# Layer norm and RWKV head norm of a two-layer encoder trunk with their GpSimd steps moved to VectorE and ScalarE

## The chip, the cores and the metric

The kernel runs on one core of one Trainium2 chip. The metric is the device time of one execution in microseconds (us), the median of several runs. The engines of the core work on instruction queues of their own: TensorE (PE; PEld is its weight load), VectorE (DVE), ScalarE (ACT), GpSimd (POOL), and SyncE (SP), which here issues the DMA transfers.

## The reference, cut to what matters

Two layers run over 2560 tokens (2048 of one request and 512 of another) of width 1024. Both layers end with an output projection, a gated residual and a layer norm over the 1024 channels; layer 1 also has RWKV-7 heads, whose output gets a norm over the 64 channels of each head.

```python
def layer_norm(x, g, b, eps=1e-5):
    mu = jnp.mean(xf, axis=-1, keepdims=True)
    var = jnp.mean(jnp.square(xf - mu), axis=-1, keepdims=True)
    return ((xf - mu) * lax.rsqrt(var + eps) * g + b).astype(x.dtype)
...
# end of rwkv7_time_mix
mu = jnp.mean(o, axis=-1, keepdims=True)
var = jnp.mean(jnp.square(o - mu), axis=-1, keepdims=True)
o = ((o - mu) * lax.rsqrt(var + RWKV_LN_EPS)).reshape(bsz, seq, D_W) * lnx_w + lnx_b
return (o + bonus.reshape(bsz, seq, D_W)) * jax.nn.silu(g.astype(jnp.float32))
...
# end of each layer
y = jnp.concatenate([c_out, d_out], axis=-1) @ w_out
return residual_post_norm(x, gate, y, ln_g, ln_b)   # layer_norm(ALPHA * x + (1 + gate) * y)
```

## The kernel before

The tokens are cut into 5 blocks of 512. Values that go into a matmul at higher precision are split in two: ScalarE copies x to a rounded `hi`, and another engine writes `lo = x - hi`; the matmul is then a sum of products of the parts (three for an output projection).

The stages follow one another: layer 0 (input projection, HGRN2 and GLA heads), its output projection `out_proj(0)` (1493 to 1745 us of the profiled execution), the input projection of layer 1 (to some 2640 us), the core of layer 1 with attention and the RWKV scan (to some 3800 us), and `out_proj(1)` (to the end).

`out_proj` works on tiles of 128 tokens, 20 in all. For a tile it loads `oh` and `ol` (the parts of the heads' output) and `xt` (the residual), does 48 matmuls of 512 columns into two halves `pp` (three buffers), and for each half runs three DVE instructions: `y = pp * gt`, `y = ALPHA * xt + y`, and the norm's statistics. Then `ln_tail` follows for the whole row: a few instructions on one column for mean and reciprocal deviation, the normalization in one DVE instruction (L357), and multiply by `lng` and add of `lnb`, the lower 512 channels on DVE and the upper 512 on POOL. In `out_proj(0)` the result is written to memory, transposed on PE, modulated (`h`), split (`h1s`, whose `lo` is computed on POOL) and written as input of layer 1; in `out_proj(1)` it is the output.

`rwkv_post` is the head norm. It runs once for each of 4 pairs of heads and each block, 20 times, on tiles of 128 channels by 512 tokens (all named `ptmp`): two loads, their sum (POOL), split (ACT, POOL), a matmul with `cmean` that subtracts the head's mean, copy and square (ACT, DVE), split (ACT, POOL), a matmul with `bmean` for the variance, `Ln` and `Exp` on ACT for the reciprocal root, a square on POOL and two DVE instructions that refine it, multiply and affine step on DVE, add of the bonus (POOL), multiply by the gate (DVE), and `out_split` (ACT, POOL) with two writes to `o_scr`.

Work is interleaved by generators in lanes: each `tick()` advances the first generator of every lane by one `yield`. The four `rwkv_post` of the block `self.first` (block 1) run one after the other in the lane "post" at the end of the core of layer 1; the other 16 are fed by `feed1` in four lanes F0 to F3 while `out_proj(1)` runs its tiles, beginning with block 1; the tiles of a block begin, in program order, only after its four posts. The pool of `ptmp` has 20 buffers there. The final order of the instructions on each engine is set by a scheduler with a time model of its own (`schedule_with_timeline_sim=True`), which works from the program order as priority; each engine then runs its queue in that fixed order. `ln_exp()` loads the ACT function set that holds both `Ln` and `Exp` once ahead of these stages.

The helpers `tt` (two tensors, L113), `stt` (tensor, scalar, tensor; L116), `ts` (tensor, two scalars; L123) and `act` (L110) issue the instructions, so that most rows bear their lines.

Of the kernel before, what the change touches and what calls it, by code (L numbers as in the profile page):

```python
# [11 lines left out]
F32R = mybir.dt.float32r  # L12
I32 = mybir.dt.int32
BF16 = mybir.dt.bfloat16
AF = mybir.ActivationFunctionType
ALU = mybir.AluOpType
# [24 lines left out]
class Common:  # L41
# [303 lines left out]
    def ln_tail(self, b, t, y, st, lng, lnb, emit_tile, pools):  # L345
        nc = self.nc
        sm = pools[1]
        mv = sm.tile([128, 2], F32, tag="mv", name="mv")
        nc.vector.bn_aggr(mv, st)
        rs = sm.tile([128, 1], F32, tag="rs", name="rs")  # L350
        self.act(rs, mv[:, 1:2], AF.Ln, bias=self.eps5)
        self.act(rs, rs, AF.Exp, scale=-0.5)
        va = sm.tile([128, 1], F32, tag="va", name="va")
        self.ts(va, mv[:, 1:2], 1e-5, rs, ALU.add, ALU.mult)
        self.ts(va, va, rs, -0.5, ALU.mult, ALU.mult)
        self.stt(rs, va, 1.5, rs, ALU.add, ALU.mult)
        self.ts(y, y, mv[:, 0:1], rs, ALU.subtract, ALU.mult)  # L357
        h = slice(0, 512)
        g = slice(512, 1024)
        self.tt(y[:, h], y[:, h], lng[:, h], ALU.mult)  # L360
        self.tt(y[:, g], y[:, g], lng[:, g], ALU.mult, nc.gpsimd)
        self.tt(y[:, h], y[:, h], lnb[:, h], ALU.add)
        self.tt(y[:, g], y[:, g], lnb[:, g], ALU.add, nc.gpsimd)
        yield
        yield from emit_tile(b, t, y, pools)


class Even(Common):
# [197 lines left out]
        self.out_split(y, col, b)  # L566
        yield

    def out_split(self, y, col, b, pool=None):
        nc = self.nc  # L570
        yh, yl = (pool.tile([128, NB], F32R, tag=x, bufs=1 + (pool is not self.ap), name=x) if pool else self.wt(x, dt=F32R) for x in ("yh", "yl"))
        self.act(yh, y, AF.Copy)
        self.tt(yl, y, yh, ALU.subtract, nc.gpsimd)
        nc.sync.dma_start(out=self.o_scr[b, 0, :, col], in_=yh[:].bitcast(F32))
        nc.sync.dma_start(out=self.o_scr[b, 1, :, col], in_=yl[:].bitcast(F32))

# [267 lines left out]
class Odd(Even):  # L844
# [659 lines left out]
    def rwkv_post(self, p, b, pool, bufs):  # L1504

        nc = self.nc
        t1 = lambda dt=F32: pool.tile([128, NB], dt, tag="ptmp", bufs=bufs, name="ptmp")
        o, c = t1(), t1()
        nc.sync.dma_start(out=o, in_=self.acc_scr[0, p, b])
        nc.sync.dma_start(out=c, in_=self.acc_scr[1, p, b])  # L1510
        yield
        yield
        yield
        self.tt(o, o, c, ALU.add, nc.gpsimd)
        yield
        yield
        yield
        parts = self.split(o, t1(F32R), t1(F32R))
        yield
        yield  # L1520
        yield
        yield
        ps = self.psum()
        self.mm2(ps, self.cmean, parts)
        nc.scalar.copy(c, ps)
        self.tt(o, c, c, ALU.mult)
        parts = self.split(o, t1(F32R), t1(F32R))
        yield
        yield
        yield  # L1530
        yield
        ps = self.psum()
        self.mm2(ps, self.bmean, parts)
        rs = t1()
        self.act(rs, ps, AF.Ln, bias=self.eps64)
        self.act(rs, rs, AF.Exp, scale=-0.5)
        u = t1()
        self.tt(u, rs, rs, ALU.mult, nc.gpsimd)
        nc.sync.dma_start(out=o, in_=self.bv_scr[p, b])
        yield  # L1540
        self.stt(u, ps, 64e-5, u, ALU.add, ALU.mult)
        self.stt(rs, u, 3.0, rs, ALU.subtract, ALU.mult)
        self.tt(c, c, rs, ALU.mult)
        self.ts(c, c, self.rvw[:, p:p + 1], self.rv[:, 7, p:p + 1], ALU.mult, ALU.add)
        nc.sync.dma_start(out=rs, in_=self.g_scr[p, b])
        yield
        self.tt(c, c, o, ALU.add, nc.gpsimd)
        self.tt(c, c, rs, ALU.mult)
        yield
        self.out_split(c, 4 + p, b, pool)  # L1550
        yield

    def feed1(self, order, pool):
# [206 lines left out]
```

## Time and profile before

| | us |
|---|---|
| median of 3 runs | 4163.66 (4152.8 to 4171.17) |
| the profiled execution | 4167.95 |
| its span, first to last instruction | 4166.2 |
| PE busy in it | 3743.6 (90%) |
| DVE busy | 2838.6 (68%) |
| ACT busy | 2149.8 (52%) |
| POOL busy | 1145.3 (27%) |

Busy times are merged: overlapping instructions of one engine count once. Busy time of an instruction runs from its start to its end, and so holds time in which it is held up after its start.

### The profile page before, as it was taken

What the parts mean: (1) busy time and instruction counts of PE and PEld (TensorE: products, weight loads), DVE (VectorE), ACT (ScalarE), POOL (GpSimd) and SP (SyncE); (2) the same over time, 40 slices, a digit from 0 to 9 for tenths busy, and PEclk for the clock granted to TensorE, in tenths of its full rate; (3) what the DMA queues carried; (4) which work ended last, traced back from release to release, by engine and by line L of the source; (5) the groups of instructions that cost most, each with busy time, mean ns of one, the idle gap of its engine ahead of it and who ended that gap; (6) DMA issues with size and microseconds to landing.
All of it is one profiled execution on the core that took longest, in us unless ns stands there. A gap on an engine that the chain in (4) does not pass through costs nothing. (4 is left out here: it accounts for less than half of the span.)

```text
span 4166.2 us, 75101 instructions
## 1 busy us (share of the span) xinstructions
PE 3743.6 (90%) x27864; PEld 3067.3 (74%) x27864; DVE 2838.6 (68%) x6393; ACT 2149.8 (52%) x4198; POOL 1145.3 (27%) x1403
## 2 busy tenths in 40 slices
PE   6999999999888699999999989799999999995688
PEld 4878787777666577777777768578888888874567
DVE  4554545456666669757675768778777778775898
ACT  4565656555455432245454545556566666664220
POOL 1021212112211244423333322312222211113784
PEclk8999999999999799999999999899999999996889
DMA  7644445456555388768778876744454444534665
GB/s 264 215 144 165 167 148 202 155 193 217 210 207 198 109 251 253 232 230 263 242 258 260 252 250 218 197 103 117 109 121 116 118 119 118 125 79 150 222 223 173
DMA packets 768781, 770.20 MB, mean 185 GB/s; under 512 B 341632, under 2 KB 635136, under 8 KB 742816
## 3 DMA queue, kind: packets, MB, share of 16 engines
q1 hardware_dynamic: 768416, 765.40, 57.9%
q8 instruction: 221, 3.62, 0.4%
q14 instruction: 144, 1.18, 0.1%
HBM read 535.55 MB, written 220.20 MB: 181 GB/s over the span
## 5 line engine op out<-in xcount | busy, mean ns | idle before, releaser
L126 PE MATMUL pp<-h,whi 128*128 128x512 f32 (+2 forms) x4800 | 1565.7, 405 | 82.0 <-DMA h<-h_scr 29.0
L126 PEld LDWEIGHTS pp<-h,whi 128*128 128x128 f32 (+2 forms) x4800 | 895.4, 191 | 294.3 <-DMA h<-h_scr 30.5
L126 PE MATMUL pp<-h,wlo 128*128 128x512 f32 (+2 forms) x2400 | 958.5, 400 | 4.8 <-POOL wlo L113 4.7
L126 PEld LDWEIGHTS pp<-h,wlo 128*128 128x128 f32 (+2 forms) x2400 | 456.0, 190 | 110.5 <-POOL wlo L113 7.3
L110 ACT ACT_TABLE_LOAD x227 | 291.2, 1283 | 23.1 <-DVE cl L500 10.4
L126 PE MATMUL pp<-owh,oh 128*128 128x512 f32 x640 | 259.8, 406 | 23.6 <-DMA oh<-o_scr 22.6
L126 PE MATMUL pp<-owh,ol 128*128 128x512 f32 x640 | 256.2, 402 | 9.8 <-DMA ol<-o_scr 9.8
L1319 POOL COPY LD<-GS 32x128 f32<-32x128 f32 x320 | 115.1, 360 | 524.0 <-ACT GS L1316 508.7
L126 PE MATMUL pp<-owl,oh 128*128 128x512 f32 x640 | 259.1, 405 | 0.0
L113 POOL TENSOR_TENSOR wlo<-wst,whi 128x512 fp32r<-128x512 f32 (+3 forms) x87 | 161.0, 1856 | 248.4 <-ACT whi L110 244.8
L113 POOL TENSOR_TENSOR at<-abuf,abuf 64x256 f32<-64x256 f32 x80 | 63.7, 796 | 517.9 <-DVE abuf L530 448.3
L126 PE MATMUL gram<-KR,Zc 128*128 128x128 f32 x1280 | 188.5, 287 | 5.5 <-DMA KR<-z_scr 2.5
L126 PE MATMUL fin<-GB,SW 128*128 128x128 f32 x1280 | 179.4, 282 | 11.0 <-ACT OH L1433 8.1
L113 POOL TENSOR_TENSOR tmp<-tmp 128x512 fp32r<-128x512 f32 x80 | 116.6, 1457 | 256.6 <-ACT tmp L110 209.4
L113 DVE TENSOR_TENSOR SS<-chain,OH 64x64 f32<-64x64 f32 x608 | 135.1, 222 | 70.8 <-PE chain L126 59.5
L126 PEld LDWEIGHTS gram<-KR,Zc 128*128 128x128 f32 x1280 | 170.6, 201 | 8.6 <-ACT R L1334 3.1
L126 PEld LDWEIGHTS fin<-GB,SW 128*128 128x128 f32 x1280 | 161.2, 195 | 16.4 <-ACT OH L1433 11.4
L113 POOL TENSOR_TENSOR ptmp<-ptmp 128x512 f32<-128x512 f32 (+1 forms) x100 | 141.8, 1430 | 82.5 <-ACT ptmp L110 26.5
L126 PEld LDWEIGHTS pp<-owh,oh 128*128 128x128 f32 x640 | 125.5, 196 | 52.6 <-DMA oh<-o_scr 21.7
L110 ACT ACTIVATE S<-chain,ecol 128x128 f32<-128x128 f32 x320 | 115.4, 367 | 89.4 <-PE chain L141 86.0
L126 PEld LDWEIGHTS pp<-owh,ol 128*128 128x128 f32 x640 | 124.7, 195 | 37.7 <-DMA ol<-o_scr 11.7
L126 PE MATMUL chain<-RX,S 128*128 128x128 f32 x608 | 134.6, 310 | 14.0 <-DVE od L113 7.8
(327 smaller groups left out, 8330.5 us busy)
## 6 DMA issues: line engine op xcount, KB each, us to landing
h<-h_scr SPq DMA_DIRECT2D x70, 2048.0 KB, 9.2
h<-h_scr SPq DMA_DIRECT2D x80, 1024.0 KB, 7.4
z_scr<-Z SPq DMA_DIRECT2D x40, 1024.0 KB, 4.8
h_scr<-h SPq DMA_DIRECT2D x10, 2048.0 KB, 7.6
oh<-o_scr SPq DMA_DIRECT2D x40, 512.0 KB, 5.6
ol<-o_scr SPq DMA_DIRECT2D x40, 512.0 KB, 6.6
h_scr<-h1s SPq DMA_DIRECT2D x20, 1024.0 KB, 5.4
Zc<-z_scr SPq DMA_DIRECT2D x80, 256.0 KB, 3.2
```

The source lines that it names most:

```text
L110: self.nc.scalar.activation(out=out, in_=in_, func=func, bias=bias, scale=scale)
L113: (eng or self.nc.vector).tensor_tensor(out=out, in0=a, in1=b, op=op)
L126: self.nc.tensor.matmul(out=out, lhsT=lhsT, rhs=rhs, start=start, stop=stop)
L1319: nc.gpsimd.tensor_copy(LD[blk, cs], gs[blk, :, 32 * i:32 * i + 32])
```

## The change

The layer norm's tail becomes two DVE instructions over the whole row of 1024: `(y - mean) * lng`, then `y * rs + lnb`. In `rwkv_post` no instruction is left on POOL: the first sum, the `lo` of the two splits, the add of the bonus and the `lo` of the output split go to DVE; the square of the centred value goes from DVE to ACT and reads the matmul's PSUM; the square of the reciprocal root goes from POOL to ACT; the affine step goes from DVE to ACT. The number and order of the yields are unchanged. `out_split` of layer 0, the split of `h1s` and the weight splits stay on POOL.

```diff
-        self.ts(y, y, mv[:, 0:1], rs, ALU.subtract, ALU.mult)
-        h = slice(0, 512)
-        g = slice(512, 1024)
-        self.tt(y[:, h], y[:, h], lng[:, h], ALU.mult)
-        self.tt(y[:, g], y[:, g], lng[:, g], ALU.mult, nc.gpsimd)
-        self.tt(y[:, h], y[:, h], lnb[:, h], ALU.add)
-        self.tt(y[:, g], y[:, g], lnb[:, g], ALU.add, nc.gpsimd)
+        self.stt(y, y, mv[:, 0:1], lng, ALU.subtract, ALU.mult)
+        self.stt(y, y, rs, lnb, ALU.mult, ALU.add)
...
-    def out_split(self, y, col, b, pool=None):
+    def out_split(self, y, col, b, pool=None, eng=None):
...
-        self.tt(yl, y, yh, ALU.subtract, nc.gpsimd)
+        self.tt(yl, y, yh, ALU.subtract, eng or nc.gpsimd)
...
-        self.tt(o, o, c, ALU.add, nc.gpsimd)
+        self.tt(o, o, c, ALU.add)
...
-        parts = self.split(o, t1(F32R), t1(F32R))
+        parts = self.split(o, t1(F32R), t1(F32R), nc.vector)
...
-        self.tt(o, c, c, ALU.mult)
-        parts = self.split(o, t1(F32R), t1(F32R))
+        self.act(o, ps, AF.Square)
+        parts = self.split(o, t1(F32R), t1(F32R), nc.vector)
...
-        self.tt(u, rs, rs, ALU.mult, nc.gpsimd)
+        self.act(u, rs, AF.Square)
...
-        self.ts(c, c, self.rvw[:, p:p + 1], self.rv[:, 7, p:p + 1], ALU.mult, ALU.add)
+        self.act(c, c, AF.Identity, bias=self.rv[:, 7, p:p + 1], scale=self.rvw[:, p:p + 1])
...
-        self.tt(c, c, o, ALU.add, nc.gpsimd)
+        self.tt(c, c, o, ALU.add)
...
-        self.out_split(c, 4 + p, b, pool)
+        self.out_split(c, 4 + p, b, pool, nc.vector)
```

## Rows read from the trace of the kernel before

**Rows 1.** Stages by --windows: length, each engine's busy us (count), granted clock, DMA.
```profile
1493.00:1750.00 257.00, 238.60 (x1092) 195.76 (x1092) 225.14 (x346) 66.04 (x153) 125.04 (x74) 0.96 0.78 243
...
3808.00:3850.00 42.00, 13.19 (x36) 8.30 (x34) 16.60 (x28) 14.25 (x19) 17.51 (x13) 0.50 0.56 189
...
3875.00:4083.60 208.60, 162.97 (x629) 126.91 (x627) 194.66 (x236) 56.59 (x108) 163.96 (x108) 0.85 0.68 222
4083.60:4154.70 71.10, 71.06 (x312) 58.44 (x312) 63.65 (x100) 3.49 (x14) 27.35 (x16) 1.00 0.53 175
```

**Rows 2.** Groups of DVE by form, 3875 to 4083.6 us: count | busy us, mean ns.
```profile
L113 DVE TENSOR_TENSOR ptmp<-ptmp 128x512 f32<-128x512 f32 x46 | 55.9, 1222 | 1.5 <-DMA ptmp<-g_scr 1.0 <-POOL ptmp L113 0.5
L116 DVE SCALAR_TENSOR_TENSOR y<-xt,y 128x512 f32<-128x512 f32 x23 | 25.8, 1122 | 0.1
L116 DVE SCALAR_TENSOR_TENSOR ptmp<-ptmp 128x512 f32<-128x512 f32 x16 | 18.5, 1160 | 0.2 <-DVE ptmp L116 0.2
L113 DVE TENSOR_TENSOR y<-pp,gt 128x512 f32<-128x512 f32 x23 | 15.6, 677 | 2.1 <-PE pp L126 2.1
L123 DVE TENSOR_SCALAR y<-y,mv,rs 128x1024 f32<-128x1024 f32 x10 | 15.3, 1533 | 0.1
...
L113 DVE TENSOR_TENSOR y<-y,lng 128x512 f32<-128x512 f32 x11 | 15.0, 1367 | 0.2
L123 DVE TENSOR_SCALAR ptmp<-ptmp,rvw,c_rvec 128x512 f32<-128x512 f32 x16 | 13.4, 841 | 0.0
L113 DVE TENSOR_TENSOR y<-y,lnb 128x512 f32<-128x512 f32 x11 | 12.9, 1172 | 0.1
```

**Rows 3.** Timeline near the end: start us, us, engine, operation.
```profile
4141.33 1.61 POOL L113 TENSOR_TENSOR y<-y,lnb 128x512 f32<-128x512 f32 x1
...
4141.72 1.77 DVE L116 SCALAR_TENSOR_TENSOR y<-xt,y 128x512 f32<-128x512 f32 x1
...
4144.85 0.69 DVE L116 SCALAR_TENSOR_TENSOR y<-xt,y 128x512 f32<-128x512 f32 x1
...
4148.66 0.69 DVE L113 TENSOR_TENSOR y<-y,lng 128x512 f32<-128x512 f32 x1
```

**Rows 4.** Waits of PE, 3875 to 4083.6 us: total us, times, longest.
```profile
PE pt L126 <- ACT ptmp L110: 19.5, 7, 9.7
PE pt L126 <- ACT ptmp L1525: 12.4, 3, 7.2
```

**Rows 5.** Groups of POOL by form, 3875 to 4083.6 us.
```profile
L113 POOL TENSOR_TENSOR ptmp<-ptmp 128x512 f32<-128x512 f32 x44 | 62.8, 1437 | 21.3 <-DVE ptmp L123 18.0 <-DMA ptmp<-acc_scr 2.3 <-DVE rs L116 0.7
L113 POOL TENSOR_TENSOR ptmp<-ptmp 128x512 fp32r<-128x512 f32 x26 | 41.3, 1593 | 10.3 <-ACT ptmp L110 9.1 <-PE pt L126 1.3
L113 POOL TENSOR_TENSOR yl<-ptmp,yh 128x512 fp32r<-128x512 f32 x16 | 26.3, 1646 | 6.5 <-ACT yh L110 6.5
```

**Rows 6.** A two-tensor DVE operation over 1024 elements, 3740 to 3855 us.
```profile
L113 DVE TENSOR_TENSOR owl<-st,owh 128x1024 fp32r<-128x1024 f32 x4 | 4.9, 1222 | 6.6 <-ACT owh L110 6.6
```

**Rows 7.** Timeline of ACT in layer 0: a logarithm and the square behind it.
```profile
1310.71 0.69 ACT L110 ACTIVATE tmp<-pt,eps 128x512 f32<-128x512 f32 x1
1311.29 0.62 ACT L110 ACTIVATE tmp<-oT 128x512 f32<-128x512 f32 x1
```

**Rows 8.** First output projection, 1493 to 1750 us: a wait of PE, a group of POOL.
```profile
PE pt L141 <- DVE y L113: 12.7, 5, 4.7
...
L113 POOL TENSOR_TENSOR h1s<-h,h1s 128x1024 fp32r<-128x1024 f32 x19 | 48.6, 2558 | 89.9 <-ACT h1s L110 69.8 <-DVE rs L116 12.9 <-DMA xt<-x 7.2
```

**Rows 9.** Timeline ahead of the second output projection's first tile.
```profile
3840.75 1.26 POOL L113 TENSOR_TENSOR ptmp<-ptmp 128x512 f32<-128x512 f32 x1
...
3845.44 2.85 SPq L324 DMA_DIRECT2D oh<-o_scr  x3
```

**Rows 10.** Timeline of the last tile's norm.
```profile
4158.38 0.81 DVE L123 TENSOR_SCALAR y<-y,mv,rs 128x1024 f32<-128x1024 f32 x1
...
4161.12 1.59 POOL L113 TENSOR_TENSOR y<-y,lnb 128x512 f32<-128x512 f32 x1
```

## The prediction

> **What bounds the kernel now.** The change touches two output projections and the 20 head norms, so I first cut the span into stages and read busy times and clock of each [rows 1]. In the first output projection PE is busy for 238.6 of 257.0 us: PE sets the pace, and DVE (225.1) is close behind. In the second, from 3875.0 to 4083.6 us, while the 16 fed head norms run, DVE is busy for 194.7 of 208.6 us and PE for 163.0 at a mean granted clock of 0.85 (1.00 is 2.4 GHz, 0.50 the lower level of 1.2 GHz): DVE is the limit. From 4083.6 to 4154.7 PE is busy all the time at 1.00, with 312 matmuls in 71.1 us, 0.228 us each; a tile of 48 costs PE 10.9 us there.
>
> The second view is DVE's groups in the DVE-bound stretch [rows 2]. The same kind of instruction has very different means: 1222 ns for two `ptmp` of 512 elements, 677 ns for `pp` times `gt`, whose first input lies in PSUM. The timeline tells why [rows 3]: the residual add takes 0.69 us when POOL is idle and 1.77 us when POOL's instruction of 1.61 us started just before it; it ends only after POOL's has ended. So the stretched instructions are those with two inputs in SBUF (and the one-input normalization, 1533 ns on average against 0.81 us alone [rows 2, 10]), and much of DVE's "busy" time is time held up by POOL. POOL is busy for 164.0 of these 208.6 us [rows 1].
>
> Last, PE's waits in that stretch [rows 4]: two groups, 31.9 us, are matmuls of head norms that wait for ACT, at the end of chains that run through POOL and DVE. PE works in order, so the tiles' matmuls stand behind them.
>
> **Part 1: the head norms and norms between 3875 and 4083.6 us.** I sum DVE's instructions that the change touches, before and after, for the same work.
>
> Before: 55.9 + 25.8 + 18.5 + 15.3 + 15.0 + 13.4 + 12.9 = 156.8 us [rows 2], without the PSUM group, which stays.
>
> After: two-tensor instructions of 512: 46, less the 14 that square (16 norms need three each, two stay: 46 - 32), plus those from POOL: 44 + 26 + 16 less 16 squares of the root, 70 [rows 5]. That is 102. With POOL idle each costs 0.69 us [rows 3]: 70.4 us. The 23 residual adds and 16 refining steps at 0.69: 15.9 + 11.0. The affine step costs nothing: it goes to ACT, busy for 56.6 of 208.6 us; with three more instructions of some 0.62 us for each of 16 norms [rows 7] that becomes 86, so ACT has room. If this cover were gone, 16 x 1.9 = 30 us. The layer norm has 21 whole-row instructions (half of the three groups of 10, 11 and 11 makes 10.7 tiles, two each). The trace has no such instruction of 1024; from below the normalization alone, 0.81 [rows 10], from above twice the 512 one, 1.38 [rows 3]. I take 1.22, which two tensors of 1024 cost [rows 6], as both new ones read two tensors: 25.6 us (17 to 29). Together 70.4 + 15.9 + 11.0 + 25.6 = 122.9. DVE gains 33.9 us (31 to 43 with the bounds).
>
> Not all of it becomes time. PE's 629 matmuls at 0.228 us are 143 us, so PE with its 31.9 us of waits needs 175 of what would be 208.6 - 33.9 = 175: both engines would be at the limit at once. The chains get shorter too (five steps of 1.4 to 1.6 us on POOL [rows 5] become 0.69 or 0.62), which should shorten those waits. I take 26 us; 0 if PE's waits stay and DVE's gain only becomes idle time, 43 at most.
>
> A rule speaks against the layer norm's new form. The Trainium skill, VectorE: DVE Perf Modes, "The perf-mode tier table", gives fp32 `tensor_scalar` two elements per cycle and two-tensor instructions one. Uncontended that agrees with the trace (0.81 us for 1024 elements of the one, 1.22 of the other): old 0.81 + 0.69 + 0.69 = 2.19 us per tile on DVE, new 2.44, so by that rule alone the 40 tiles would lose 10 us of DVE time. The old three have means that add up to 4.07 instead [rows 2].
>
> **Part 2: the first output projection.** PE waits five times, 12.7 us, for the norm's result before it can transpose [rows 8]. The two POOL instructions on the way go; the split of `h1s` stays on POOL (19 of 2.56 us, 48.6 of 125.0 us) and can still hold up a DVE instruction per tile. So the norm gets faster but not always. I take 9 us of the 12.7; bounds 0 and 13. What is late next is DMA, 0.78 busy, and PE itself.
>
> The Trainium skill, SBUF - State Buffer, "Who interferes with whom", says that a DVE instruction with two SBUF inputs and a GpSimd one that reads SBUF exclude each other for the whole instruction. The trace agrees (1.77 us behind 1.61). By this rule `h1s` could hold each tile's DVE queue by up to 2.56 us, as it can now.
>
> **Part 3: the start of the second output projection.** From 3808 to 3850 us PE is busy for 13.2 of 42 us at a clock of 0.50, 1.2 GHz [rows 1]: the first load of `oh` [rows 9] waits for the fourth head norm of the first block, whose bonus add runs on POOL only at 3840.75. Each norm has five POOL steps of about 1.26 us; at 0.69 a norm saves 5 x 0.57 = 2.9 us. The four run one after the other, but the first ones run beside the scan's end, which has its own pace: I count two, 6 us. From below it is 0, if the projection's weights, which are loaded and split in the same time, come last; from above all four, 11.
>
> **Part 4: the last tile.** From 4158.38 to 4162.71 us (POOL's end) is 4.33 [rows 10]; two instructions of 1.22 make 2.44. It saves 2 us (1 to 3), nothing hides it.
>
> **The sum.** 26 + 9 + 6 + 2 = 43 us from the profiled execution's 4167.95: 4125. That execution was 4.3 us above the median, within the spread of the runs (18.4 us); I forecast 4123 us.
>
> **Rivals.** *Gain does not arrive.* DVE gets idle, but the chains over ACT and PE, now all in queues of busy engines, keep the pace, and in the first projection DMA (0.78) does. Then parts 3 and 4 and some of part 2 remain, about 11 us: 4157. For it: PE's 31.9 us of waits name ACT as the last [rows 4]; against it: ACT itself is only 27% busy, it waited for POOL and DVE.
>
> *PE becomes the only limit.* If the waits vanish with the locks and the clock recovers from 0.85 to 1.00, the stretch costs the 143 us of its matmuls and, estimated, 7 more: 58 instead of 26, 4093. For it: the clock falls only where PE waits; against it: order and chains remain.
>
> *DVE stalls for ACT: slower.* Five DVE steps of each norm now follow directly behind an ACT instruction in a fixed order (three `lo`, the refining step, the bonus add). If nothing is queued between, DVE stands still and with it the evacuation of `pp`, for which PE waits. 16 x 5 = 80 waits; one ACT instruction each (0.62) costs 50 us, two (1.24) 99. It decides (slower by 21 us) from (34 + 17 + 21) / 80 = 0.9 us per wait; at 1.24, 4168 - 17 - 34 + 99 = 4216. For it: the queue order is fixed ahead by a time model; against it: four lanes and the tiles give other work, and now only 14 of 208.6 us are idle.
>
> *The stretch is not POOL's.* If two-input instructions cost 1.22 us anyway, the sum after becomes 102 x 1.22 + 25.8 + 18.5 + 21 x 2.44 = 220 instead of 156.8: 4168 + 63 = 4231. Against it: 0.69 and 1.77 us for the same instruction [rows 3].
>
> *Function table.* Should `Square` not be in the loaded set, each norm would load tables. A square starts 0.58 us behind a logarithm, with no load between [rows 7]; little is left of it. With two loads in each of 20 norms, each estimated at two ACT instructions (1.24 us), it would cost 50 us of ACT time; its idle time hides about half, which leaves 4123 + 25 = 4148.
>
> **Chances.** Forecast (4100 to 4143) 0.56; PE the limit 0.13; gain does not arrive 0.19; DVE stalls 0.07; stretch not POOL's 0.03; tables 0.02. A measurement of this kernel tells about 0.5% (21 us) from no change. Faster by more: 0.56 + 0.13 + 0.03 of the gain that does not arrive = 0.72; within: 0.16 of that, 0.01 of the stalls and 0.01 of the tables, 0.18; slower: 0.10. The range goes from 4084 (PE the limit, parts 2 and 3 at their upper bounds) to 4165 (gain does not arrive, with 8 us of stall); it leaves out 0.1 above and some 0.06 below. The forecast alone has 4100 to 4143.
>
> **What would show it.** Between the start of the first tile and the end of the fed head norms DVE's two-tensor instructions of 512 have a mean near 0.69 us, the whole-row ones near 1.22, and POOL is all but empty; that stretch is some 26 us shorter and the PE-bound rest about as long as now; PE's waits for `y` in the first projection fall from 12.7 to about 4 us; the first `oh` load comes some 6 us sooner after the scan's end. The prediction is wrong if DVE shows many waits of 0.6 us and more for ACT in the fed stretch, if the matmuls of the head norms make PE wait longer than 31.9 us, if the scheduler puts the stages in another order so that other stages move by more than 10 us, or if whole-row instructions take over 1.4 us with POOL idle.

## The result, and the profile after

The changed kernel takes 4101.78 us (median of 4 runs, 4089.63 to 4110.71) against 4166.76 us for the kernel before beside it: a ratio of 0.9848, 95% interval 0.9811 to 0.9884, so 65 us faster. The forecast was 4123, with a range of 4084 to 4165. The profiled execution took 4097.39 us, its span is 4095.5.

First the stages of the kernel after (the windows: length, then busy time and count of PE, PEld, DVE, ACT and POOL, granted clock, DMA share, GB/s): the first output projection, the hand-over behind the scan, and the second output projection with the fed head norms and without.

```profile
1456.00:1723.00 267.00, 250.62 (x1149) 206.00 (x1148) 205.71 (x343) 78.70 (x167) 78.04 (x40) 0.97 0.84 255
3801.00:3821.00 20.00, 11.55 (x39) 9.20 (x39) 5.62 (x19) 5.73 (x8) 0.69 (x1) 0.59 1.05 329
3840.00:4015.00 175.00, 157.25 (x651) 126.17 (x650) 158.11 (x276) 85.06 (x154) 2.39 (x1) 0.94 0.82 272
4015.00:4086.00 71.00, 71.00 (x314) 58.77 (x314) 53.82 (x91) 3.87 (x16) 0.00 (x0) 1.00 0.55 178
```

The third row answers to the 208.6 us of [rows 1]: POOL's 164.0 us of work are gone (2.4 left), DVE's fell from 194.7 to 158.1, the clock rose from 0.85 to 0.94, and the stretch is 33.6 us shorter. The last 71 us, where PE is busy all the time, are as long as before. The groups of DVE in that third row:

```profile
L113 DVE TENSOR_TENSOR ptmp<-ptmp 128x512 f32<-128x512 f32 x60 | 39.4, 680 | 2.2 <-DMA ptmp<-g_scr 2.1
L113 DVE TENSOR_TENSOR y<-pp,gt 128x512 f32<-128x512 f32 x26 | 17.6, 681 | 6.4 <-DMA y<-y 4.3 <-PE pp L126 2.1
L113 DVE TENSOR_TENSOR ptmp<-ptmp 128x512 fp32r<-128x512 f32 x26 | 17.4, 678 | 0.7 <-ACT ptmp L110 0.6
L116 DVE SCALAR_TENSOR_TENSOR y<-xt,y 128x512 f32<-128x512 f32 x25 | 16.9, 680 | 0.0
...
L116 DVE SCALAR_TENSOR_TENSOR y<-y,mv,lng 128x1024 f32<-128x1024 f32 x11 | 14.0, 1274 | 0.0
L116 DVE SCALAR_TENSOR_TENSOR y<-y,rs,lnb 128x1024 f32<-128x1024 f32 x10 | 12.6, 1265 | 0.0
L116 DVE SCALAR_TENSOR_TENSOR ptmp<-ptmp 128x512 f32<-128x512 f32 x16 | 12.0, 747 | 0.1
...
L113 DVE TENSOR_TENSOR yl<-ptmp,yh 128x512 fp32r<-128x512 f32 x16 | 10.8, 678 | 0.3 <-ACT yh L110 0.3
...
L116 DVE SCALAR_TENSOR_TENSOR rs<-va,rs 128x1 f32<-128x1 f32 x11 | 1.5, 140 | 0.0
```

Instructions with two inputs of 512 elements in SBUF, 1122 to 1222 ns before [rows 2], take 678 to 680 ns, as much as the one that reads PSUM (`y<-pp,gt`, 681); the refining step fell from 1160 to 747. Next, PE's waits and then DVE's in the same stretch (total us, times, longest):

```profile
PE pp L126 <- DMA ol<-o_scr: 11.3, 2, 8.9
PE pp L126 <- ACT owh L110: 3.5, 2, 3.2
...
PE pt L126 <- DVE ptmp L116: 0.3, 1, 0.3
```

```profile
DVE ptmp L116 <- ACT ptmp L110: 7.3, 3, 2.9
...
DVE ptmp L113 <- ACT ptmp L110: 0.6, 1, 0.6
DVE yl L113 <- ACT yh L110: 0.3, 1, 0.3
```

The 31.9 us in which PE stood before the head norms' matmuls [rows 4] are 0.3 us. PE's longest waits are now for the load of `ol`, twice, 11.3 us (5.0 in the stretch before); the rest is mostly for the projection's weights (`owh`, `owl`). DVE waits for `ptmp` and `yh` of ACT 5 times, 8.2 us in all. The load of `ol` stands behind the head norms too, since it reads what they write (DMA queue's waits, same stretch):

```profile
SPq L325 <- DMA o_scr<-yl: 7.4, 3, 3.5
```

To compare whole kernels I cut each span at four starts: that of the first matmul of layer 1's input projection (`pp<-h`), of the last scan step (`S<-chain`), and of the first and the last `pp<-owh,ol` matmul of the second output projection. The table has one execution of each kernel. "Core" is the input projection and core of layer 1, "stretch" all the tiles of the second output projection. The rows for the kernel after, and its first load of `oh` (start us, us):

```profile
L110 ACT ACTIVATE S<-chain,ecol x320: 344/367/418, 2725.0 to 3800.7; 128x128 f32<-128x128 f32 x160
```

```profile
3804.62 1.78 SPq L324 DMA_DIRECT2D oh<-o_scr  x2
```

| profiled execution | us | to layer 1 | core | hand-over | stretch | last | DVE busy in stretch |
|---|---|---|---|---|---|---|---|
| before | 4167.9 | 1738.3 | 2068.6 | 48.6 | 298.8 | 11.9 | 267.8 |
| **after** | 4097.4 | 1723.1 | 2077.6 | 20.3 | 265.0 | 9.5 | 219.8 |
| after again (e12) | 4101.0 | 1729.4 | 2076.4 | 19.9 | 263.9 | 9.5 | |
| e1 layer norm only | 4116.5 | 1723.0 | 2070.9 | 32.0 | 278.9 | 9.9 | 248.5 |
| e2 head norm only | 4120.1 | 1737.9 | 2065.7 | 37.2 | 265.3 | 12.2 | 236.2 |
| e3 POOL reads added | 4138.8 | 1727.7 | 2094.7 | 25.0 | 278.7 | 10.8 | 259.9 |
| e4 POOL memsets added | 4113.9 | 1724.4 | 2093.1 | 26.7 | 258.4 | 9.5 | 218.1 |
| e5 before, one column more | 4175.5 | 1737.3 | 2076.4 | 48.9 | 298.9 | 11.9 | |
| e6 norm in three on DVE | 4118.2 | 1720.8 | 2090.8 | 26.9 | 267.0 | 10.9 | 231.3 |
| e7 head norm all on DVE | 4107.5 | 1723.0 | 2077.0 | 19.8 | 276.1 | 9.9 | 245.3 |
| e8 norm steps left out | 4081.8 | 1726.2 | 2080.5 | 20.7 | 247.2 | 5.3 | 177.2 |
| e9 `h1s` on DVE | 4108.3 | 1715.5 | 2096.5 | 26.2 | 258.8 | 9.5 | |
| e10 two weight buffers | 4140.9 | 1728.9 | 2116.1 | 23.5 | 261.1 | 9.5 | |
| e11 both | 4135.3 | 1726.3 | 2112.5 | 23.4 | 261.9 | 9.5 | |

From before to after: -15.2, +9.0, -28.3, -33.8 and -2.4, together -70.7, the difference of the two spans. The hand-over gave far more than forecast. The core, in which the change touches only the four head norms at its end, took longer in this execution; e5 shows that this is hardly more than two executions of one order differ.

### The profile page after: what moved, and what is told of

Read it like the earlier page. It is cut to its first block, busy times and chain, and to the rows that moved or that the text cites. A ratio compares the mean times of both kernels' runs of the same rounds, so it can differ in the third digit from the quotient of the medians.

```text
span 4095.5 us, 74774 instructions
## 1 busy us (share of the span) xinstructions
PE 3723.6 (91%) x27864; PEld 3055.2 (75%) x27864; DVE 2758.2 (67%) x6413; ACT 2186.7 (53%) x4258; POOL 861.0 (21%) x1203
## 5 line engine op out<-in xcount | busy, mean ns | idle before, releaser
L126 PE MATMUL pp<-owl,oh 128*128 128x512 f32 x640 | 256.0, 400 | 2.3 <-DVE owl L113 1.8
L126 PEld LDWEIGHTS gram<-KR,Zc 128*128 128x128 f32 x1280 | 169.5, 199 | 11.3 <-issue 5.6
L110 ACT ACTIVATE S<-chain,ecol 128x128 f32<-128x128 f32 x320 | 116.6, 368 | 75.7 <-PE chain L141 72.8
L126 PE MATMUL chain<-RX,S 128*128 128x128 f32 x608 | 137.3, 312 | 13.7 <-DVE od L113 10.9
L126 PEld LDWEIGHTS pp<-owh,oh 128*128 128x128 f32 x640 | 123.3, 193 | 33.5 <-ACT owh L110 4.4
L126 PEld LDWEIGHTS pp<-owl,oh 128*128 128x128 f32 x640 | 123.8, 193 | 29.2 <-DVE owl L113 2.7
## 6 DMA issues: line engine op xcount, KB each, us to landing
Zc<-z_scr SPq DMA_DIRECT2D x80, 256.0 KB, 3.2
```

The lines of the kernel that those rows point to most:

```text
L110: self.nc.scalar.activation(out=out, in_=in_, func=func, bias=bias, scale=scale)
L126: self.nc.tensor.matmul(out=out, lhsT=lhsT, rhs=rhs, start=start, stop=stop)
```

## The experiments

**e1 and e2: each half alone.** The kernel before with the new layer norm, and the kernel after with the old one:

```diff
# e1 (e2 is the reverse, in the kernel after)
-        self.ts(y, y, mv[:, 0:1], rs, ALU.subtract, ALU.mult)
-        self.tt(y[:, h], y[:, h], lng[:, h], ALU.mult)
-        self.tt(y[:, g], y[:, g], lng[:, g], ALU.mult, nc.gpsimd)
-        self.tt(y[:, h], y[:, h], lnb[:, h], ALU.add)
-        self.tt(y[:, g], y[:, g], lnb[:, g], ALU.add, nc.gpsimd)
+        self.stt(y, y, mv[:, 0:1], lng, ALU.subtract, ALU.mult)
+        self.stt(y, y, rs, lnb, ALU.mult, ALU.add)
```

> Only the layer norm's two whole-row instructions; the head norms as before. Theory A (DVE is held up by POOL while both read SBUF; each POOL instruction taken away gives DVE its time back): the first output projection gets all of its gain, 15 us earlier start of layer 1; in the second the head norms keep POOL some 130 of 208 us busy, so DVE's two-input means there stay above 1.0 us and it gains 5 to 10 us; with 2 us at the last tile 4140 to 4145, ratio 0.994 to 0.995. Theory B (what counts is the shorter chain of the head norms): 17 us and no more, 4149, ratio 0.996.

> Only the head norm's changes; the layer norm as before, with two POOL instructions per tile. Theory A: first output projection as before (no gain), second one some 40 us shorter, the two-input means there between 0.7 and 1.0 us as POOL keeps 3.3 us per tile: 4115 to 4125, ratio 0.988 to 0.990. Theory B: all of the 62 us from the scan's end to the last matmul come with it: 4104, ratio 0.985. If the 9 us that the core of layer 1 lost are the head norms' doing, they show here and not in the run with the layer norm alone.

Measured: e1 4119.47 us (ratio 0.9875, 0.9853 to 0.9897), e2 4131.03 (0.9904, 0.9873 to 0.9934). The windows of the stretch in e1, then in e2:

```profile
3825.90:4104.80 278.90, 253.05 (x1017) 196.25 (x1018) 248.53 (x329) 67.94 (x137) 158.41 (x97) 0.94 0.71 230
```

```profile
3840.80:4106.10 265.30, 243.83 (x1018) 196.10 (x1018) 236.22 (x395) 97.40 (x184) 67.45 (x39) 0.94 0.74 243
```

Both times lie outside what either theory gave. The layer norm alone takes 15.3 us off the time to layer 1 (theory A: 15) and 19.9 off the stretch (5 to 10); the head norm alone takes 33.5 off the stretch (40), as much as both together. So the two savings overlap there: with the head norms off POOL, the 67 us of the old layer norm that stay on POOL cost the stretch little. How little is not told exactly, as the kernels with the whole change's work in the stretch differ among themselves (258.8 to 265.0 us). The longer core shows in neither half (+2.3 and -2.9). The hand-over adds up: head norms -11.4 (before to e2) and -11.7 (e1 to after), layer norm -16.6 and -16.9. No term of mine had a layer norm act on the hand-over, where none runs. In e1 the scan and the first load of `oh` stand so:

```profile
L110 ACT ACTIVATE S<-chain,ecol x320: 346/368/414, 2725.6 to 3793.9; 128x128 f32<-128x128 f32 x160
```

```profile
3723.30 1.27 POOL L113 TENSOR_TENSOR ptmp<-ptmp 128x512 f32<-128x512 f32 x1 [11.24 <-DVE SS L113]
...
3814.67 2.77 SPq L324 DMA_DIRECT2D oh<-o_scr  x3
```

The first head norm starts 70.6 us ahead of the last scan step; in the kernel before it was 53.6 us (3753.3 and 3806.9). It is the order of the queues that changed: the scheduler had planned the whole of layer 1 anew behind the edited norm. The kernel before and e2 have one order through the core up to its last part, with a head start of 53.6 and 57.6 us; e1, the kernel after and e7 have another, with 70.6 to 75.7 us. The 17.0 us between e1 and the kernel before are about what the hand-over gained.

**e3 and e4: POOL's work put back, with and without reads.** The kernel after, with two unused POOL instructions added to every half tile; they differ in nothing else, and PE's order is the same but for a few instructions.

```diff
+                        nc.scalar.copy(junk[:, 0:1], st[:, hf, 0:1])
+                        for _ in range(2):
+                            self.tt(junk2, junk, junk, ALU.add, nc.gpsimd)   # e3
+                            nc.gpsimd.memset(junk, 0.0)                      # e4 instead
```

> The changed kernel with four POOL additions of 128x512 on two scratch tiles put back for each tile of both output projections (160 in all, some 1.3 us each; ACT writes one column of the scratch tile after each half's statistics, so that they come in the tiles' rhythm). They compute nothing that is used. Theory A: DVE's two-input instructions beside them grow from 0.68 to a mean of 0.9 to 1.2 us, the whole-row ones from 1.28 to over 1.6; the first projection loses 8 to 15 us again and the second 10 to 25: 4120 to 4140. Theory B: within 5 us of the changed kernel, 4097 to 4107.

> As the run with POOL's additions, but the 160 POOL instructions are memsets of the scratch tile, which read nothing. If any work of POOL holds DVE up, means and time are as with the additions, scaled by the memsets' length. If only POOL instructions that read SBUF do, DVE's means stay at 0.68 and 1.28 us and the time within 6 us of the changed kernel's 4102. The Trainium skill, SBUF - State Buffer, Who interferes with whom, says the latter for instructions with two SBUF inputs.

Measured: e3 4132.64 us (0.9901, 0.9868 to 0.9934), e4 4110.1 (0.9847, 0.9820 to 0.9875). Groups of POOL and DVE in the stretch of e3, then of e4:

```profile
L113 POOL TENSOR_TENSOR junk<-junk 128x512 f32<-128x512 f32 x77 | 107.1, 1391 | 156.0 <-ACT junk L345 136.9 <-PE pp L126 16.1
...
L116 DVE SCALAR_TENSOR_TENSOR y<-xt,y 128x512 f32<-128x512 f32 x39 | 34.5, 894 | 0.3
L116 DVE SCALAR_TENSOR_TENSOR y<-y,rs,lnb 128x1024 f32<-128x1024 f32 x19 | 31.4, 1655 | 0.2
```

```profile
L347 POOL MEMSET junk<- 128x512 f32 x78 | 41.0, 526 | 201.3 <-ACT junk L345 199.1
...
L116 DVE SCALAR_TENSOR_TENSOR y<-xt,y 128x512 f32<-128x512 f32 x39 | 26.4, 685 | 0.3
L116 DVE SCALAR_TENSOR_TENSOR y<-y,rs,lnb 128x1024 f32<-128x1024 f32 x19 | 24.3, 1278 | 0.2
```

Nobody reads the added instructions' result; ACT's copy into `junk` waits for them, 12.0 us in e3 and 6.0 in e4. Where they read SBUF, DVE's two-input instructions above get 209 and 377 ns longer (the other whole-row one only 63) and the stretch takes 278.7 instead of 258.4 us; where they only write, DVE is as fast as with POOL idle. The lock is shown as a cause by itself. The memsets are also shorter (41 us against 107), so the comparison is not of equal POOL time; but in proportion to it one would expect, as an estimate, 80 and 144 ns, and the means are within 6 ns of the kernel after's 684 and 1272. The Trainium skill, SBUF — State Buffer, "Who interferes with whom", names exactly this line between a GpSimd instruction that reads SBUF and one that only writes it; the two runs agree. Two expectations failed: the first projection, where theory A gave 8 to 15 us, is at 1727.7 in e3, within the two profiles of the kernel after, and e4 took 8 us more than the kernel after instead of at most 6, with 15.5 us in its core.

**e5: meant as a re-plan with nothing in it.** The kernel before, with one DVE memset of one column in the layer norm.

```diff
+        nc.vector.memset(sm.tile([128, 1], F32, tag="nud", name="nud"), 0.0)
```

> The kernel before with one memset of one column on DVE (some 0.07 us) added to each layer-norm tail and nothing else; it moves the scheduler's clock a little, and the order of the core of layer 1 behind it comes out otherwise. Theory C (part of the measured change is the order that the scheduler writes after any edit): from the first matmul of layer 1 to the scan's last step it takes not 2068.6 us, as before, but up to 25 us more or less, and from there to the first tile not 48.6 but 30 to 60; the first output projection stays within 3 us and the fed stretch within 10. Theory D (the order does not matter): every stage within 4 us, total within 6 us of before.

Measured: 4176.79 us (1.0014, 0.9998 to 1.0030). The core is 7.8 us longer, hand-over and stretch are within 0.3 us. But nothing was planned anew: compared one by one, the core's 2525 instructions of ACT, 948 of POOL and 1670 DMA issues of SyncE stand in the same order in the two traces, and DVE's differ by the memset alone. So e5 does not test theory C. It shows the spread: with one order the core took 2068.6 and 2076.4 us in two executions. The change's +9.0 is hardly clear of that.

What an order is worth is read from the others. Up to its last 80 us, where the head norms run, the core has one order, a few neighbours aside, in each of these groups:

| one order of the core | core, us |
|---|---|
| before, e2, e5 | 2065.7 to 2076.4 |
| after, after again, e1, e7 | 2070.9 to 2077.6 |
| e3, e4, e6 | 2090.8 to 2094.7 |
| e10, e11 | 2112.5 to 2116.1 |

e8 (2080.5) and e9 (2096.5) have an order each. The first two groups overlap, so nothing shows that the change's order made the core longer. The last two lie 13 to 50 us above them, clear of the spread, though the core's work up to there is the same: there the order is the cause.

**e6: fusion or POOL.** The kernel after, with the norm in three whole-row instructions, all on DVE.

```diff
-        self.stt(y, y, mv[:, 0:1], lng, ALU.subtract, ALU.mult)
-        self.stt(y, y, rs, lnb, ALU.mult, ALU.add)
+        self.ts(y, y, mv[:, 0:1], rs, ALU.subtract, ALU.mult)
+        self.tt(y, y, lng, ALU.mult)
+        self.tt(y, y, lnb, ALU.add)
```

> The changed kernel with the layer norm in the old three steps, but each over the whole row and all on DVE: normalization 0.81 us, multiply and add 1.22 to 1.28 each, 3.35 us per tile in place of 2.57. Theory A (POOL's absence is what pays): the first output projection is as short as in the changed kernel (layer 1 starts within 3 us of 1723), since DVE has 40 us free there; the stretch from the first tile to the last matmul within 6 us of 265; the last tile 0.8 us longer. Rival (the fusion into two instructions pays): the first projection 8 us or more longer than in the changed kernel. Core and hand-over may come out otherwise by the order.

Measured: 4119.48 us (0.9883, 0.9864 to 0.9902). Its three norm instructions in the stretch:

```profile
L113 DVE TENSOR_TENSOR y<-y,lnb 128x1024 f32<-128x1024 f32 x19 | 23.2, 1219 | 0.0
L113 DVE TENSOR_TENSOR y<-y,lng 128x1024 f32<-128x1024 f32 x19 | 23.1, 1215 | 0.2
...
L123 DVE TENSOR_SCALAR y<-y,mv,rs 128x1024 f32<-128x1024 f32 x19 | 15.4, 809 | 0.2
```

They are 3.24 us a tile where the fused pair is 2.54. Yet the time to layer 1 is 1720.8, not longer, and the stretch 267.0, 2.0 longer; the last tile costs 1.4 more. The remaining loss, 13.2 us in the core and 6.6 in the hand-over, lies where the edited norm does not run: e6 has the order of e3 and e4, whose cores are as long. What pays is that POOL is out, not that two instructions replace three.

**e7: squares and affine step back on DVE.**

```diff
-        self.act(o, ps, AF.Square)
+        self.tt(o, c, c, ALU.mult)
-        self.act(u, rs, AF.Square)
+        self.tt(u, rs, rs, ALU.mult)
-        self.act(c, c, AF.Identity, bias=self.rv[:, 7, p:p + 1], scale=self.rvw[:, p:p + 1])
+        self.ts(c, c, self.rvw[:, p:p + 1], self.rv[:, 7, p:p + 1], ALU.mult, ALU.add)
```

> The changed kernel with the squares and the affine step of the head norm on DVE and not on ACT: three more DVE instructions per norm, 0.69 + 0.69 + 0.54 us, 31 us for the 16 fed norms. Core order as in the changed kernel. Theory E (the stretch is now PE's, DVE has slack): from first tile to last matmul 265 to 275 us, total within 8 us of 4102. Rival (DVE still sets the stretch): 280 to 296 us, total 4117 to 4133.

Measured: 4111.75 us (0.9866, 0.9849 to 0.9882). The stretch:

```profile
3819.80:4095.80 276.00, 248.20 (x1017) 197.53 (x1018) 245.32 (x425) 69.28 (x137) 3.98 (x1) 0.92 0.72 236
```

DVE works 25.5 us more than in the kernel after, and the stretch is 11.1 us longer, just outside theory E's 265 to 275 and short of its rival's 280. The core's order is that of the kernel after and its time within 0.6 us, so giving ACT these steps is worth about 11 us.

**e8: the norm's two instructions left out.** The kernel after without its two whole-row instructions; the rows stay unnormalized.

```diff
-        self.stt(y, y, mv[:, 0:1], lng, ALU.subtract, ALU.mult)
-        self.stt(y, y, rs, lnb, ALU.mult, ALU.add)
```

> The changed kernel without the layer norm's two whole-row instructions, so that the rows stay unnormalized: DVE loses 2.57 us per tile, 51 us in each output projection. Theory E (both projections are now PE's): layer 1 starts no more than 4 us sooner than 1723, the stretch from first tile to last matmul stays within 8 us of 265; only the last tile gets 2.6 us shorter. Rival (DVE still sets them): 15 to 50 us shorter. Core and hand-over may come out otherwise by the order.

Measured: 4079.07 us (0.9785, 0.9771 to 0.9800). The stretch:

```profile
3827.40:4074.60 247.20, 239.46 (x1018) 194.49 (x1018) 177.23 (x339) 96.96 (x185) 2.38 (x1) 0.97 0.80 264
```

The time to layer 1 is not shorter (1726.2): there the norm is wholly hidden behind PE now. The stretch loses another 17.8 us for 42.5 us less of DVE's busy time: DVE still sets part of it. Its clock of 0.97 says little, as the two profiles of the kernel after have 0.95 and 0.94 there at about one length. The theory that the stretch is PE's alone falls. Over the nine kernels with both numbers in the table, the stretch follows DVE's busy time roughly, at some half a microsecond for one (estimated by a straight line, which single kernels miss by up to 11 us): 247.2 at 177.2, 265.0 at 219.8, 276.1 at 245.3, 298.8 at 267.8.

**e9, e10, e11 and e12: the last POOL instruction, the weights, and the kernel after again.**

```diff
# e9, in out_proj(0)
-             self.tt(hs[:, :, 1], h, hs[:, :, 0], ALU.subtract, nc.gpsimd)
+             self.tt(hs[:, :, 1], h, hs[:, :, 0], ALU.subtract)
# e10, staging of the projection's weights; e11 has both
-             ws = self.pool(ctx, f"ows{l}", bufs=1)
+             ws = self.pool(ctx, f"ows{l}", bufs=2)
```

> The kernel after, with the last POOL instruction beside the first output projection's tiles, the lo part of h1s, moved to DVE as well (20 instructions of 1024 elements). Theory A (DVE is held up beside a reading POOL instruction): the first output projection can only lose what PE still idles there, 9 of 237 us, so at most 5 us, 4097 us by the profiled execution if the core keeps its length; DVE gains no idle time, because 20 x 1.22 us come to it and the 20 locks of up to 2.5 us go. Rival B (POOL's separate instruction was cover, not cost): 24 us more of DVE work in a stretch where DVE is busy for 196 of 237 us makes the first projection 5 to 20 us longer. Either way the core of layer 1 is planned anew behind the edit and may move by -8 to +26 us, so the verdict is read in the first projection alone.

> The kernel after, with two buffers in place of one for staging the output projection's weights, which are loaded, rounded and split one slab after the other. Theory C (behind the scan's end it is now the weights that PE waits for, not the head norms): the hand-over of 20.3 us becomes 5 to 12 us shorter, or the first tile of the stretch starts as before and runs 5 to 12 us faster. Rival D (the head norms of the first block still come last): hand-over and stretch within 3 us of 20.3 and 265.0. The core may move by -8 to +26 us by the new plan.

> Both edits of the two kernels before: the lo part of h1s on DVE and two staging buffers for the weights. If both help by themselves and the core is planned no worse than in the kernel after, 4085 to 4097 us; if the plan of the core costs what it did in other re-planned kernels (13 to 17 us more), 4100 to 4115.

> The kernel after once more, unchanged, beside the three others on the same chip: 4090 to 4111 us, a ratio to the kernel before of 0.981 to 0.988. It measures how far a stage moves with no edit at all: every stage within 3 us of the first profile if stages are told by the order alone; more if a part of the differences read so far is spread between executions.

Measured on one chip: e9 4101.76 us (0.9836, 0.9804 to 0.9869), e10 4140.01 (0.9930, 0.9905 to 0.9955), e11 4134.85 (0.9916, 0.9884 to 0.9948), the kernel after again 4102.46 (0.9839, 0.9806 to 0.9872). None beats the kernel after, and e11 missed both of its ranges.

The second profile of the kernel after is alike within 1.2 us in every stage but the first, which took 1729.4 instead of 1723.1: differences of 6 us there are spread between executions.

e9 is at 1715.5 at layer 1, 7.6 and 13.9 us ahead of the two profiles of the kernel after, more than either theory gave, and loses it in the core (2096.5). DVE's groups in the first output projection, kernel after and then e9:

```profile
L116 DVE SCALAR_TENSOR_TENSOR y<-xt,y 128x512 f32<-128x512 f32 x40 | 30.8, 775 | 1.2
L116 DVE SCALAR_TENSOR_TENSOR rs<-va,rs 128x1 f32<-128x1 f32 x20 | 28.4, 1421 | 0.6
```

```profile
L116 DVE SCALAR_TENSOR_TENSOR y<-xt,y 128x512 f32<-128x512 f32 x39 | 27.2, 699 | 0.6
...
L113 DVE TENSOR_TENSOR h1s<-h,h1s 128x1024 fp32r<-128x1024 f32 x19 | 23.2, 1220 | 5.4 <-ACT h1s L110 5.4
...
L116 DVE SCALAR_TENSOR_TENSOR rs<-va,rs 128x1 f32<-128x1 f32 x20 | 3.1, 156 | 0.3
```

DVE took over 23.2 us of `h1s` and is still busy for less time, 185.4 us instead of 196.0 between 1495 and 1732 us: the instruction on one column alone gave back 25.3. Rival B falls.

e10's hand-over and stretch are 284.6 us together; in the two profiles of the kernel after they are 285.3 and 283.8. Theory C falls: a second buffer brings nothing there. The core got 38.5 us longer, outside the range given, with e11 alike (34.9): the two share an order that no other kernel has.

## Why the prediction was right, and where its steps were off

**Part 1, the sum for DVE: right. What of it becomes time: too little.** I worked out 122.9 us for DVE's changed instructions. In the stretch after, the same groups (102 two-tensor instructions, 25 residual adds, 16 refining steps, 21 whole-row ones) have 67.6 + 16.9 + 12.0 + 26.6 = 123.1 us. That it comes so close is partly luck: the first term is 2.8 us below mine and the others are 1.0 each above. The whole-row instruction, for which the trace of before had no row, took 1.27 us (taken: 1.22). The sum left out the one-column `rs<-va,rs`, which POOL held up as well: in the stretch before it took 6.0 us, in the one after 1.5.

```profile
L116 DVE SCALAR_TENSOR_TENSOR rs<-va,rs 128x1 f32<-128x1 f32 x10 | 6.0, 601 | 0.2
```

The step that failed is the discount from 33.9 to 26: "PE with its 31.9 us of waits needs 175". Those waits did not stay in part, they went: 0.3 us are left, and 6.3 more for the load of `ol` took their place. Over the whole stretch PE's waits before the head norms' matmuls are 37.6 us in the kernel before, 18.8 in e1 and 6.7 in e2: either half of the change takes a good part of them, the head norms' more. The stretch gave 33.8. That it lies no lower is DVE and PE together, as e7 and e8 show from both sides. The affine step on ACT took 0.81 us instead of 0.62; what that cost was not measured by itself.

**Part 2, right in mechanism, a little small.** PE's wait for the norm's result, in the waits of PE from 1456 to 1723 us:

```profile
PE pt L141 <- DVE y L116: 2.9, 1, 2.9
```

It fell from 12.7 [rows 8] to 2.9 (3.3 in the second profile), 9.8 us, where I took 9. The stage gave 15.2 us in one execution and 8.9 in the other. Over the seven profiles with the whole norm on DVE and `h1s` on POOL (both of the kernel after, e1, e3, e4, e6, e7) layer 1 begins at 1724.5 on average, over the three with the old norm (before, e2, e5) at 1737.8: 13.3, just past my upper bound. What goes beyond the waits is PE's clock, for which I had no term: from the first tile to layer 1 the same matmuls keep PE busy for 256.0 us at 0.94 before and 251.0 at 0.97 after (254.3 at 0.95 in the second profile, which began layer 1 later).

```profile
1456.10:1738.30 282.20, 256.04 (x1150) 209.54 (x1150) 229.91 (x361) 78.54 (x167) 130.12 (x78) 0.94 0.79 242
```

```profile
1455.60:1723.10 267.50, 251.02 (x1149) 206.40 (x1150) 205.81 (x343) 79.10 (x167) 78.54 (x40) 0.97 0.84 255
```

The stated limit, that `h1s` would go on holding DVE, was right, and larger than I knew (e9).

**Part 3: the largest miss.** I counted two of four head norms, 6 us, with 11 as the bound; e2 against the kernel before and the kernel after against e1 give 11.4 and 11.7 for them, as much as all four at the 2.9 us that I took for one. The other 16.6 us came with the layer norm edit, through another order of the queues, and no term held them. In the kernel before PE waits 18.7 us for `oh`, behind the last head norm:

```profile
3850.17 0.80 PE L126 MATMUL pp<-owh,oh 128*128 128x512 f32 x1 [18.72 <-DMA oh<-o_scr]
```

In the kernel after the last head norm's last DVE instruction starts 0.4 us before the last scan step. The gate rows, which `gt` needs, and the load of `ol` now fill the hand-over:

```profile
3806.56 5.96 PE L126 MATMUL pt<-dg,allones 128*128 128x128 f32 x20 [2.93 <-DVE dg L121]
...
3820.97 0.80 PE L126 MATMUL pp<-owh,ol 128*128 128x512 f32 x1 [5.24 <-DMA ol<-o_scr]
```

Core and hand-over together moved by -19.3. Over all the kernels this sum lies between 2096 (the kernel after again) and 2140 (e10). So a part of the gain hangs on this plan, which for the prediction is luck, and another edit can lose it. Why the scheduler starts the first head norm earlier with the new norm is open.

**Part 4: right.** 2.4 us against 2. The two instructions of the last tile, with the reciprocal root between:

```profile
4088.86 1.28 DVE L116 SCALAR_TENSOR_TENSOR y<-y,mv,lng 128x1024 f32<-128x1024 f32 x1
...
4090.74 1.28 DVE L116 SCALAR_TENSOR_TENSOR y<-y,rs,lnb 128x1024 f32<-128x1024 f32 x1
```

**The rivals.** The gain arrived, so 4157 fell. PE did not become the only limit: the clock of the fed stretch is 0.94, and e8 still takes 17.8 us from the stretch. DVE's head norm steps wait for ACT 5 times and not 80. The stretch was POOL's (e3). The function tables are loaded 227 times through `act` (L110) in both kernels. From the sum's 4125 to the two profiles of the kernel after it is 24 to 28 us: 8 to 9 in the stretch, 0 to 6 up to layer 1, 13 to 15 in hand-over and core together.

**The price of the new form.** The pair takes 2.54 us of DVE a tile where the old three, held up by POOL, took 4.07 [rows 2]. The Trainium skill, VectorE: DVE Perf Modes, "The perf-mode tier table", gives fp32 `tensor_scalar` twice the rate of two-tensor instructions. For 1024 elements e6 has 0.81 and 1.22 us, the same way round but a factor of 1.5. So with nothing to hold either up the old form would be the cheaper one (0.81 + 0.69 + 0.69 us against 2.54), and it is the lock that outweighs this.

## What to carry to other kernels

Where an engine is the limit, ask first how much of its busy time is its own: the same instruction at 0.69 and 1.77 us in one trace points to a lock, e3 and e4 are a way to test for it, and the other engine's work was then cheaper on the busy engine than beside it. Price the chains with the engine: PE's waits in a stretch may be the same lock seen from further off, and go with it. And where a scheduler plans the whole program, a local edit can move distant stages: in two of its orders the core here takes 13 to 39 us more than in the kernel after. So read the result stage by stage, compare kernels of one order, and look in the trace whether the order did change, before a difference is put down to it: e5's had not.

## What was not expected of the hardware

A DVE instruction on one column can be held until POOL's instruction ends, as one on a whole row can. In the first output projection of the kernel after, POOL reads SBUF for 3.15 us, and the timeline has:

```profile
1603.28 3.15 POOL L113 TENSOR_TENSOR h1s<-h,h1s 128x1024 fp32r<-128x1024 f32 x1 [8.62 <-ACT h1s L110]
```

```profile
1604.58 1.87 DVE L116 SCALAR_TENSOR_TENSOR rs<-va,rs 128x1 f32<-128x1 f32 x1
```

The `rs` instruction, with two inputs of one column, ends at 1606.45, POOL's at 1606.43; with POOL idle it takes 0.16 us (e9). Of the twenty in this projection, 15 end within 0.02 us of POOL's instruction. Together they cost 28.4 us of DVE; in e9 they cost 3.1, and the 25.3 between are more than the 23.2 that the work on POOL costs DVE when it does it itself. With the fused norm the hold grew: in the kernel before the same twenty took 9.4 us (1495 to 1745 us), in e6, with the norm in three instructions, 300 ns each.

```profile
L116 DVE SCALAR_TENSOR_TENSOR rs<-va,rs 128x1 f32<-128x1 f32 x20 | 9.4, 471 | 0.6
```
